# Attention's softmax by entire heads: scores of two heads in one five-bank PSUM tile, one maximum, one exponential and one scaling per head

## The chip, the cores and the metric

The kernel runs on one core of a Trainium2 chip. It is one launch of a long program (36247 instructions in the profiled execution) and the metric is its device time in microseconds (us), the median of three runs. Five engines work side by side and meet only at semaphores: TensorE (PE in the profile, with its weight loads as PEld), VectorE (DVE), ScalarE (ACT), GpSimd (POOL) and SyncE (SP, which only issues transfers here). Each works through its own instructions in the order in which they were written down. PSUM, into which TensorE writes, has eight banks of 512 fp32 numbers per partition.

## The reference, cut to what matters

The reference is a whole network block: a mixer with a state-space half and an attention half, a mixture of experts, then a second block. Only the attention is touched. It has 16 query heads and 4 key/value heads of 64 numbers, 1024 query positions and 256 + 1024 = 1280 key positions (context and latent), all in fp32:

```
q = rope(rms_norm(q));  k = [k_ctx, rope(rms_norm(k))];  v = [v_ctx, v]
for a block of 128 queries, for each of 16 heads (4 heads share one k, v):
    s = q . k                      # 128 x 1280
    p = exp(s - max(s)) / sum(exp(s - max(s)))
    o = p @ v
```

The result must be close to fp32, so the kernel holds most matrices as a sum of two fp32r numbers (a high and a low part), and multiplies both.

## The kernel before, in words

`attention` handles 8 blocks of 128 queries times 4 key heads, so 32 groups. A group has four query heads, that is two pairs of heads, and 10 chunks of 128 keys. The work is written as one loop over steps `s`, and in each step one piece of several stages is issued, each stage with its own distance from `s`; the loop runs under a manual schedule, so on TensorE, ScalarE, VectorE and GpSimd the written order is the executed order.

The front half runs ahead by `AHEAD` steps and is counted by `n = s + AHEAD`. Five values of `n` make a pair of heads, k = 0 to 4. `products` (L1135) writes the scores of piece k into a PSUM bank: pieces 0 and 1 are keys 0 to 511 and 512 to 1023 of the pair's first head, piece 2 holds the last 256 keys of both heads side by side in one bank, pieces 3 and 4 are keys 0 to 1023 of the second head. Each of the five banks is a tile of its own (S0 to S4). Each piece takes two matmuls (piece 2 four smaller ones), for the query's high and low parts. One step later `maxima` takes the maximum of that bank on VectorE (L1146 and L1148) and, at k = 2 and 4, the maximum over the head's three partial ones (L1155). Four steps after the product `exps` (L1170) computes the exponentials of the bank on ScalarE and sums them; GpSimd adds the three sums of a head (L1174, L1175). Five steps after it `norms` inverts the sum on VectorE (L1183) and scales the head's two halves on GpSimd (L1185).

The back half is counted by `s`, ten steps to a group. `transposes` (L1194) turns chunk `s + 2` of the four heads in one PSUM tile `pt` (two of them take turns); `high` (L1199, ScalarE) and `low` (L1203, VectorE) split it into two parts; `values` (L1215, L1216) multiplies both with v into the one bank `pv`. In a group's last step `evacuate` (L1223, L1224) copies `pv` out on ScalarE, and GpSimd adds its halves.

On TensorE a usual step is: products of piece k, transposes of a chunk, two matmuls of `values`. PSUM is full: five banks for scores, two for `pt`, one for `pv`.

Of the kernel before, what the change touches and what calls it, by code (L numbers as in the profile page):

```python
# [10 lines left out]
F = mybir.dt.float32  # L11
# [3 lines left out]
AF = mybir.ActivationFunctionType  # L15
OP = mybir.AluOpType
AX = mybir.AxisListType
# [5 lines left out]
L = 1024  # L23
S = 256
T = S + L
NB = L // 128
# [139 lines left out]
class Kernel:  # L166
# [126 lines left out]
    def conditioned(self, sm, s5_steps, zp, whp, wlp, wsp, toks):  # L293
# [11 lines left out]
        with es:  # L305
# [11 lines left out]
            for k in range(8):  # L317
# [35 lines left out]
    def proj_tok(self, sm):  # L353
# [10 lines left out]
        with es:  # L364
# [5 lines left out]
            s5_steps = self.s5_prepare(s5p, s5, pps)  # L370
            toks = [slice(S + tb * 128, S + tb * 128 + 128) for tb in range(NB)]
            wz, first = self.conditioned(sm, s5_steps, zp, whp, wlp, wsp, toks[:6])
# [14 lines left out]
            def product(wt, tok):  # L387
                return products(wt, [tok])[0]
# [113 lines left out]
            for hb in range(2):  # L502
                wt = load_block(1 + hb)
                for tb in range(NB):
                    ps = product(wt, slice(S + tb * 128, S + tb * 128 + 128))
                    next(mod)
# [596 lines left out]
    def attention(self):  # L1103
        nc, tc = self.nc, self.tc
        V = nc.vector
        self.o_es = ExitStack()
        op = self.o_es.enter_context(tc.tile_pool(name="oT", bufs=1, reuse_waits="tile"))
        self.oT = oT = [op.tile([128, 8, 128], F, name=f"oT{b}") for b in range(NB)]
        es = ExitStack()
        with es:  # L1110
            pool = lambda name, bufs=1, **kw: es.enter_context(tc.tile_pool(name=name, bufs=bufs, reuse_waits="tile", **kw))
            wp, cp, pp = pool("at_w", 2), pool("at_c"), pool("at_ps", 1, space=PS)
            kS, qS = self.kS, self.qS
            vS = cp.tile([128, NBT, 512], R, name="vS")
            nc.sync.dma_start(vS[:].bitcast(F), self.vv[:].rearrange("b p n -> p b n").bitcast(F))

            PIECES = (((0, 0, 512),), ((0, 512, 1024),), ((0, 1024, 1280), (1, 1024, 1280)), ((1, 0, 512),), ((1, 512, 1024),))
            AHEAD = 17
            NG = 4 * NB
            P, split, pvs, bank = {}, {}, {}, {}  # L1120
            mx, neg, tot, rt = {}, {}, {}, {}

            def products(n):

                pair, k = divmod(n, 5)
                b, j, p = pair // 8, pair % 8 // 2, pair % 2
                if pair >= 2 * NG:
                    return
                if n % 40 == 30 and b + 1 < NB:
                    self.load_q(b + 1)  # L1130
                S = bank[n] = pp.tile([128, 512], F, name=f"S{k}")
                o = 0
                for e, a, z in PIECES[k]:
                    for m in range(2):
                        nc.tensor.matmul(S[:, o:o + z - a], qS[b][:, 4 * j + 2 * p + e, :], kS[4 * m + j][:, a:z], start=m == 0, stop=m == 1)  # L1135
                    o += z - a

            def maxima(n):
                pair, k = divmod(n, 5)
                if n < 0 or pair >= 2 * NG:  # L1140
                    return
                if k == 0:
                    mx[pair] = wp.tile([128, 2, 3], F, name="mx")
                m = mx[pair]
                if k == 2:
                    V.tensor_reduce(m[:, :, 2], bank[n].rearrange("p (e n) -> p e n", e=2), axis=AX.X, op=OP.max)  # L1146
                else:
                    V.tensor_reduce(m[:, k // 3, k % 3:k % 3 + 1], bank[n], axis=AX.X, op=OP.max)  # L1148
                if k in (2, 4):
                    e = k // 2 - 1  # L1150
                    h = 2 * pair + e

                    hd = wp.tile([128, 8], F, name="hd", bufs=6)
                    neg[h], tot[h], rt[h] = hd[:, 0:1], hd[:, 1:4], hd[:, 4:6]
                    V.tensor_reduce(neg[h], m[:, e, :], axis=AX.X, op=OP.max, negate=True)  # L1155

            def exps(n):

                pair, k = divmod(n, 5)
                if n < 0 or pair >= 2 * NG:  # L1160
                    return
                o = 0
                for e, a, z in PIECES[k]:
                    h = 2 * pair + e
                    half = int(a > 0)
                    if (h, half) not in P:
                        P[h, half] = wp.tile([128, 768 if half else 512], F, name=f"P{half}", bufs=9 if half else 6)
                    i = k - 2 * e
                    x = P[h, half][:, a - 512 * half:z - 512 * half]
                    nc.scalar.activation(x, bank[n][:, o:o + z - a], AF.Exp, bias=neg[h], accum_out=tot[h][:, i:i + 1])  # L1170
                    o += z - a
                    if k == 2 + 2 * e:
                        r = rt[h]
                        nc.gpsimd.tensor_add(r[:, 0:1], tot[h][:, 0:1], tot[h][:, 1:2])  # L1174
                        nc.gpsimd.tensor_add(r[:, 1:2], r[:, 0:1], tot[h][:, 2:3])  # L1175

            def norms(n):
                pair, k = divmod(n, 5)
                if n < 0 or pair >= 2 * NG or k not in (2, 4):
                    return  # L1180
                h = 2 * pair + k // 2 - 1
                r = rt[h]
                V.reciprocal(r[:, 0:1], r[:, 1:2])  # L1183
                for half in range(2):
                    nc.gpsimd.tensor_scalar(P[h, half], P[h, half], r[:, 0:1], 1.0, op0=OP.mult, op1=OP.mult)  # L1185

            def transposes(n):
                g, c = divmod(n, NBT)
                if n < 0 or g >= NG:
                    return  # L1190
                pt = pp.tile([128, 4, 128], F, name="pt", bufs=2)
                o = 128 * (c - 4 if c > 3 else c)
                for i in range(4):
                    nc.tensor.transpose(pt[:, i, :], P[4 * g + i, int(c > 3)][:, o:o + 128], self.ident)  # L1194
                split[n] = pt, wp.tile([128, 4, 128], R, name="ph", bufs=4), wp.tile([128, 4, 128], R, name="pl", bufs=4)

            def high(n):
# [31 lines left out]
            with tc.manual_schedule(engines={ET.PE, ET.Activation, ET.DVE, ET.Pool}):  # L1229
                for s in range(-AHEAD, NBT * NG):  # L1230
                    n = s + AHEAD
                    last = s >= 0 and s % NBT == NBT - 1
                    if last:
                        values(s)
                    products(n)
                    maxima(n - 1)
                    transposes(s + 2)
                    low(s + 1)
                    exps(n - 4)
                    if last:  # L1240
                        evacuate(s)
                    norms(n - 5)
                    high(s + 2)
                    if not last:
                        values(s)
# [1466 lines left out]
```

## Time and profile before

| | |
|---|---|
| median of 3 runs | 2743.65 us (2742.18 to 2745.04) |
| profiled execution, its own time | 2740.33 us |
| its span, first to last instruction | 2738.4 us |
| mean granted TensorE clock | 0.959 |
| busy: TensorE, VectorE, ScalarE, GpSimd | 2536.7, 1951.2, 1336.1, 976.5 us |
| attention, first score product to last copy of `pv` | 800 to 1295 us |

The attention takes about 18% of the span. Busy times of matmuls overlap, since they are pipelined; so how fast TensorE moves is better read from the distance between the starts of matmuls than from their durations. Idle time stands in brackets in the timeline, with the instruction that ended it. `[0.43 <-ACT P L1170]` is 0.43 us in which the engine did nothing until an exponential was done.

### The profile page before, as it was taken

What the parts mean: (1) busy time and instruction counts of PE and PEld (TensorE: products, weight loads), DVE (VectorE), ACT (ScalarE), POOL (GpSimd) and SP (SyncE); (2) the same over time, 40 slices, a digit from 0 to 9 for tenths busy, and PEclk for the clock granted to TensorE, in tenths of its full rate; (3) what the DMA queues carried; (4) which work ended last, traced back from release to release, by engine and by line L of the source; (5) the groups of instructions that cost most, each with busy time, mean ns of one, the idle gap of its engine ahead of it and who ended that gap; (6) DMA issues with size and microseconds to landing.
All of it is one profiled execution on the core that took longest, in us unless ns stands there. A gap on an engine that the chain in (4) does not pass through costs nothing.

```text
span 2738.4 us, 36247 instructions
## 1 busy us (share of the span) xinstructions
PE 2536.7 (93%) x12369; PEld 2000.4 (73%) x12369; DVE 1951.2 (71%) x3735; ACT 1336.1 (49%) x2788; POOL 976.5 (36%) x1128
## 2 busy tenths in 40 slices
PE   7899999998899999998997999689799999999898
PEld 4676778854677777776775777577577788887787
DVE  7655676689649898897566777675647878775755
ACT  3233453456529999998223455343444333333433
POOL 5612011166016666666334455100241345443000
PEclk9999999988999999999987999899899999999999
DMA  7556421000610000002317788631312445547653
GB/s 270 175 189 204 155 71 39 32 8 1 245 62 17 17 17 32 17 1 69 116 70 221 223 263 264 215 109 46 112 54 74 164 148 184 173 159 269 232 196 116
DMA packets 141113, 344.21 MB, mean 126 GB/s; under 512 B 21200, under 2 KB 41344, under 8 KB 132064
## 3 DMA queue, kind: packets, MB, share of 16 engines
q1 hardware_dynamic: 88752, 198.03, 21.0%
q0 software_dynamic: 24176, 102.39, 11.5%
q10 hardware_dynamic: 28000, 41.46, 4.4%
q8 instruction: 98, 1.61, 0.2%
q14 instruction: 87, 0.71, 0.1%
HBM read 257.64 MB, written 93.62 MB: 128 GB/s over the span
## 4 chain that ended last, share of the span: by engine, by line
PE 64%; DVE 16%; ACT 7%; DMA 6%; issue 5%; POOL 2%; SPq 0%; ACTq 0%; DVEq 0%; POOLq 0%
PE m L217 5%; PE mm L215 5%; PE m L215 5%; PE m L216 5%; PE mm L217 5%; PE mm L216 5%; PE S L1135 5%; PE pt L1194 4%; PE a L216 3%; PE a L217 3%; PE a L215 2%; ACT P L1170 2%; PE pv L1215 2%; PE pv L1216 2%; PE cv L216 2%
## 5 line engine op out<-in xcount | busy, mean ns | idle before, releaser
L1203 DVE TENSOR_TENSOR pl<-pt,ph 128x512 fp32r<-128x512 f32 x320 | 219.1, 685 | 51.7 <-ACT ph L1199 46.3
L1170 ACT ACTIVATE P<-S,hd 128x512 f32<-128x512 f32 (+1 forms) x384 | 238.0, 624 | 1.8 <-DVE hd L1155 1.8
L1185 POOL TENSOR_SCALAR P<-P,hd 128x512 f32<-128x512 f32 (+1 forms) x256 | 202.7, 805 | 90.1 <-DVE hd L1183 85.5
L1135 PE MATMUL S<-kS,qS 128*128 128x512 f32 (+1 forms) x768 | 210.9, 372 | 19.1 <-ACT P L1170 19.1
L1199 ACT CAST ph<-pt 128x512 fp32r<-128x512 f32 x320 | 187.7, 587 | 28.0 <-PE pt L1194 14.5
L1194 PE MATMUL pt<-consts,P 128*128 128x128 f32 x1280 | 193.5, 273 | 6.0 <-DVE pl L1203 4.9
L1194 PEld LDWEIGHTS pt<-consts,P 128*128 128x128 f32 x1280 | 156.6, 140 | 45.2 <-DVE pl L1203 8.9
L1148 DVE TENSOR_REDUCE mx<-S 128x1 f32<-128x512 f32 x256 | 173.6, 679 | 3.0 <-PE S L1135 2.2
L1135 PEld LDWEIGHTS S<-kS,qS 128*128 128x128 f32 x768 | 128.3, 190 | 63.9 <-ACT P L1170 42.9
L1215 PE MATMUL pv<-ph,vS 128*128 128x512 f32 x320 | 151.3, 473 | 0.9 <-ACT ph L1199 0.3
L600 DVE SCALAR_TENSOR_TENSOR acc<-cv,vcol,acc 128x254 f32<-128x254 f32 (+5 forms) x288 | 110.3, 432 | 51.6 <-ACT acc L602 49.2
L2632 ACT CAST oh<-st 128x1024 fp32r<-128x1024 f32 x77 | 80.5, 1053 | 109.8 <-PE a L217 41.9
L216 PE MATMUL a<-ol,oh 128*128 128x512 f32 x308 | 122.0, 396 | 10.9 <-DVE ol L2633 10.9
L2633 DVE TENSOR_TENSOR ol<-st,oh 128x1024 fp32r<-128x1024 f32 x77 | 93.4, 1235 | 52.0 <-ACT oh L2632 45.1
L1216 PE MATMUL pv<-pl,vS 128*128 128x512 f32 x320 | 126.8, 396 | 0.2 <-DVE pl L1203 0.2
L217 PE MATMUL a<-oh,ol 128*128 128x512 f32 x308 | 121.7, 395 | 0.0
L215 PE MATMUL a<-oh 128*128 128x512 f32 x308 | 117.3, 391 | 0.3 <-DVE u L2550 0.3
L2440 ACT CAST gh<-gst 128x512 fp32r<-128x512 f32 x88 | 54.6, 621 | 128.1 <-PE m L216 122.0
L216 PE MATMUL mm<-wl,hH 128*128 128x512 f32 x288 | 114.6, 398 | 2.2 <-DVE wl L255 2.0
L215 PE MATMUL mm<-wh,hH 128*128 128x512 f32 x288 | 115.4, 401 | 0.0
L217 PE MATMUL mm<-wh,hL 128*128 128x512 f32 x288 | 113.5, 394 | 0.0
L217 PE MATMUL cv<-hH,wl 128*128 128x512 f32 (+1 forms) x288 | 104.0, 361 | 1.0 <-POOL wl L584 1.0
(785 smaller groups left out, 7494.5 us busy)
## 6 DMA issues: line engine op xcount, KB each, us to landing
gst<-in_ffn_gu_dram SPq DMA_DIRECT2D x88, 256.0 KB, 3.3
st<-hop SPq DMA_DIRECT2D x77, 256.0 KB, 7.4
wmod<-in_w_mod_dram ACTq DMA_DIRECT2D x64, 256.0 KB, 4.0
hop<-h POOLq DMA_DIRECT2D x44, 256.0 KB, 2.6
d<-in_ffn_down_dram SPq DMA_DIRECT2D x22, 512.0 KB, 3.5
wop<-d POOLq DMA_DIRECT2D x22, 512.0 KB, 3.5
st<-wop SPq DMA_DIRECT2D x44, 256.0 KB, 5.0
wst<-in_w_in_dram SPq DMA_DIRECT2D x40, 256.0 KB, 3.6
```

The costliest lines, as they stand in the source:

```text
L215: nc.tensor.matmul(out, lh, rh, start=first, stop=False)
L216: nc.tensor.matmul(out, lh, rl, start=False, stop=False)
L217: nc.tensor.matmul(out, ll, rh, start=False, stop=last)
L1135: nc.tensor.matmul(S[:, o:o + z - a], qS[b][:, 4 * j + 2 * p + e, :], kS[4 * m + j][:, a:z], start=m == 0, stop=m == 1)
L1148: V.tensor_reduce(m[:, k // 3, k % 3:k % 3 + 1], bank[n], axis=AX.X, op=OP.max)
L1170: nc.scalar.activation(x, bank[n][:, o:o + z - a], AF.Exp, bias=neg[h], accum_out=tot[h][:, i:i + 1])
L1185: nc.gpsimd.tensor_scalar(P[h, half], P[h, half], r[:, 0:1], 1.0, op0=OP.mult, op1=OP.mult)
L1194: nc.tensor.transpose(pt[:, i, :], P[4 * g + i, int(c > 3)][:, o:o + 128], self.ident)
L1199: nc.scalar.copy(split[n][1], split[n][0])
L1203: V.tensor_sub(split[n][2], split[n][0], split[n][1])
L1215: nc.tensor.matmul(pv, v, ph, start=c == 0, stop=False)
L1216: nc.tensor.matmul(pv, v, pl, start=False, stop=c == NBT - 1)
```

## The change

The five tiles for scores become one tile `S` of five banks, 128 x 2 x 1280: the two heads of a pair lie behind each other without gaps, so the first head fills banks 0, 1 and half of 2, and the second the rest. The pieces are cut along the banks, so there are as many matmuls of the same sizes as before. `maxima` is now one reduction over 1280 numbers per head (L1145), negated at once; `exps` is one activation over 1280 numbers with one sum (L1151), so GpSimd has no sums to add; `norms` is one inverse (L1156) and one scaling of 1280 numbers (L1157). The probabilities of a head are one tile, eight of them in turn. The maximum comes one step, the exponential two, and the scaling three steps after the head's last product, and the loop starts 16 steps ahead instead of 17.

```diff
-            PIECES = (((0, 0, 512),), ((0, 512, 1024),), ((0, 1024, 1280), (1, 1024, 1280)), ((1, 0, 512),), ((1, 512, 1024),))
-            AHEAD = 17
+            PIECES = (((0, 0, 512),), ((0, 512, 1024),), ((0, 1024, 1280), (1, 0, 256)), ((1, 256, 768),), ((1, 768, 1280),))
+            S = pp.tile([128, 2, T], F, name="S")
+            AHEAD = 16
...
-                S = bank[n] = pp.tile([128, 512], F, name=f"S{k}")
...
+                        nc.tensor.matmul(S[:, e, a:z], qS[b][:, 4 * j + 2 * p + e, :], kS[4 * m + j][:, a:z], start=m == 0, stop=m == 1)
+            def head(n):
+                pair, k = divmod(n, 5)
+                return None if n < 0 or pair >= 2 * NG or k not in (2, 4) else 2 * pair + k // 2 - 1
             def maxima(n):
+                h = head(n)
+                if h is not None:
+                    cols[h] = wp.tile([128, 8], F, name="hd", bufs=6)
+                    V.tensor_reduce(cols[h][:, 0:1], S[:, h % 2], axis=AX.X, op=OP.max, negate=True)
             def exps(n):
+                h = head(n)
+                if h is not None:
+                    P[h] = wp.tile([128, T], F, name="P", bufs=8)
+                    nc.scalar.activation(P[h], S[:, h % 2], AF.Exp, bias=cols[h][:, 0:1], accum_out=cols[h][:, 1:2])
             def norms(n):
+                h = head(n)
+                if h is not None:
+                    V.reciprocal(cols[h][:, 2:3], cols[h][:, 1:2])
+                    nc.gpsimd.tensor_scalar(P[h], P[h], cols[h][:, 2:3], 1.0, op0=OP.mult, op1=OP.mult)
...
-                    exps(n - 4)
+                    exps(n - 2)
...
-                    norms(n - 5)
+                    norms(n - 3)
```

How the instructions stand and what they wait for changes at three places. In the rows below the text in brackets names the engine whose semaphore the instruction waits for, and rows without one wait for nothing new. First TensorE near the start of the attention, before any transposes, so that the score products stand alone: piece 3 of the first pair is the first row, then come piece 4 and pieces 0, 1 and 2 of the second pair. Before (S_7131 is the tile of piece 3, S_7137 of piece 4, then S_7143, S_7151 and S_7161 for the next pair):

```order
L1135 MATMUL S_7131<-kS_6341,qS 128x512 [waits DVE_49]
L1135 MATMUL S_7131<-kS_6345,qS 128x512
L1135 MATMUL S_7137<-kS_6341,qS 128x512
L1135 MATMUL S_7137<-kS_6345,qS 128x512
L1135 MATMUL S_7143<-kS_6341,qS 128x512 [waits Activation_49]
L1135 MATMUL S_7143<-kS_6345,qS 128x512
L1135 MATMUL S_7151<-kS_6341,qS 128x512 [waits Activation_49]
L1135 MATMUL S_7151<-kS_6345,qS 128x512
L1135 MATMUL S_7161<-kS_6341,qS 128x256 [waits Activation_49]
```

The same place on TensorE now, with the one tile S:

```order
L1133 MATMUL S<-kS_6341,qS 128x512
L1133 MATMUL S<-kS_6345,qS 128x512
L1133 MATMUL S<-kS_6341,qS 128x512 [waits DVE_49]
L1133 MATMUL S<-kS_6345,qS 128x512
L1133 MATMUL S<-kS_6341,qS 128x512 [waits Activation_49]
L1133 MATMUL S<-kS_6345,qS 128x512
L1133 MATMUL S<-kS_6341,qS 128x512 [waits DVE_49]
L1133 MATMUL S<-kS_6345,qS 128x512
L1133 MATMUL S<-kS_6341,qS 128x256 [waits Activation_49]
```

Before, a product waited for the exponential that had read its own bank. Now pieces 4 and 1 wait for VectorE, and pieces 0 and 2 for ScalarE. Counting the semaphore's increments in the built program gives which instruction each waits for: piece 4 the maximum of the first head, piece 0 the exponential of the first head, piece 1 the maximum of the second head, piece 2 the exponential of the second head; in each case the reader of S that was issued in the step just before.

Second, VectorE in the steady part, five steps each. Before (S_8221 is a piece 2, S_8243 and S_8263 pieces 3 and 4):

```order
L1146 TENSOR_REDUCE mx<-S_8221 128x2 [waits PE_49]
L1155 TENSOR_REDUCE hd<-mx 128x1 [waits DVE_49]
L1203 TENSOR_TENSOR pl<-pt,ph 128x512 [waits Activation_49]
L1148 TENSOR_REDUCE mx<-S_8243 128x1 [waits PE_49]
L1203 TENSOR_TENSOR pl<-pt,ph 128x512 [waits Activation_49]
L1183 RECIPROCAL hd<-hd 128x1 [waits Pool_49]
L1148 TENSOR_REDUCE mx<-S_8263 128x1 [waits PE_49]
L1155 TENSOR_REDUCE hd<-mx 128x1 [waits DVE_49]
L1203 TENSOR_TENSOR pl<-pt,ph 128x512 [waits Activation_49]
L1148 TENSOR_REDUCE mx<-S_8283 128x1 [waits PE_49]
```

VectorE now, from the maximum of a first head on:

```order
L1145 TENSOR_REDUCE hd<-S 128x1 [waits PE_49,Pool_49]
L1174 TENSOR_TENSOR pl<-pt,ph 128x512 [waits DVE_49,Activation_49]
L1174 TENSOR_TENSOR pl<-pt,ph 128x512 [waits Activation_49]
L1145 TENSOR_REDUCE hd<-S 128x1 [waits PE_49,Activation_49,Pool_49]
L1174 TENSOR_TENSOR pl<-pt,ph 128x512 [waits DVE_49,Activation_49]
L1156 RECIPROCAL hd<-hd 128x1
L1174 TENSOR_TENSOR pl<-pt,ph 128x512 [waits DVE_49,Activation_49] x2
L1156 RECIPROCAL hd<-hd 128x1
```

Two reductions per pair stand where seven stood. The first head's maximum waits for TensorE, and the count says for which product: piece 3 of its pair, which lies in the second head. The second head's maximum waits for piece 0 of the next pair, and for ScalarE, namely the exponential of the first head.

Third, ScalarE in the steady part. Before, from the first exponential of a second head on (S_8329 is a piece 2):

```order
L1170 ACTIVATE P_8408,hd<-S_8329,hd 128x256
L1170 ACTIVATE P_8429,hd<-S_8329,hd 128x256 [waits DVE_49,Pool_49]
L1199 CAST ph<-pt 128x512 [waits PE_49,Activation_49]
L1170 ACTIVATE P_8448,hd<-S_8352,hd 128x512
L1199 CAST ph<-pt 128x512 [waits PE_49,Activation_49]
L1170 ACTIVATE P_8429,hd<-S_8372,hd 128x512
L1199 CAST ph<-pt 128x512 [waits DVE_49,PE_49]
```

ScalarE now, the five steps of a pair:

```order
L1151 ACTIVATE P,hd<-S,hd 128x1280 [waits DVE_49,PE_49]
L1170 CAST ph<-pt 128x512 [waits PE_49,Activation_49] x2
L1151 ACTIVATE P,hd<-S,hd 128x1280 [waits DVE_49,PE_49]
L1170 CAST ph<-pt 128x512 [waits PE_49,Activation_49] x2
L1170 CAST ph<-pt 128x512 [waits DVE_49,PE_49]
```

Six exponentials of a pair became two. Before, they waited for no product; now the first head's waits for piece 4 of its pair, and the second head's for piece 1 of the next pair. Outside the attention the engines' instructions are the same, but for the places of two weight casts on ScalarE and of one block of matmuls in the projection that follows.

## Rows read from the trace of the kernel before

**Rows 1.** Busy time by engine in the steady attention (columns: stretch, engines, clock, DMA).
```profile
820.00:1270.00 450.00, 436.73 (x2548) 352.08 (x2546) 403.69 (x851) 423.59 (x1091) 278.66 (x546) 1.00 0.05 15
```
**Rows 2.** Who waited for whom, 800 to 1300 us: total us, times, longest.
```profile
PE S L1135 <- ACT P L1170: 19.1, 35, 3.8
...
PE pt L1194 <- DVE pl L1203: 4.9, 5, 3.1
```
**Rows 3.** The line of the score products: ns min/median/max, first and last start.
```profile
L1135 PE MATMUL S<-kS,qS x768: 278/393/795, 800.3 to 1267.9; 128*128 128x512 f32 x128, 128*128 128x256 f32 x64
```
**Rows 4.** Timeline of two steps without a wait (start us, us, engine, line).
```profile
1004.58 0.73 PE L1135 MATMUL S<-kS,qS 128*128 128x256 f32 x4
...
1005.14 0.60 PE L1194 MATMUL pt<-consts,P 128*128 128x128 f32 x4
...
1005.84 0.59 ACT L1199 CAST ph<-pt 128x512 fp32r<-128x512 f32 x1 [0.17 <-PE pt L1194]
...
1006.05 0.63 PE L1135 MATMUL S<-kS,qS 128*128 128x512 f32 x2
...
1007.42 0.62 PE L1135 MATMUL S<-kS,qS 128*128 128x512 f32 x2
```
**Rows 5.** Timeline where a score product waits for an exponential.
```profile
1013.02 0.69 ACT L1170 ACTIVATE P<-S,hd 128x512 f32<-128x512 f32 x1
...
1013.60 0.20 ACT L1170 ACTIVATION_READ_ACCUMULATOR P<-S,hd 128x1 f32 x1
...
1013.85 0.72 PE L1135 MATMUL S<-kS,qS 128*128 128x512 f32 x2 [0.43 <-ACT P L1170]
...
1014.77 0.47 PE L1215 MATMUL pv<-ph,vS 128*128 128x512 f32 x1
...
1015.08 0.39 PE L1216 MATMUL pv<-pl,vS 128*128 128x512 f32 x1
```
**Rows 6.** Groups by shape, 800 to 1296 us: count, busy us, mean ns, idle before.
```profile
L1148 DVE TENSOR_REDUCE mx<-S 128x1 f32<-128x512 f32 x256 | 173.6, 679 | 3.0 <-PE S L1135 2.2
...
L1155 DVE TENSOR_REDUCE hd<-mx 128x1 f32<-128x3 f32 x128 | 20.0, 156 | 4.4
...
L1170 ACT ACTIVATE P<-S,hd 128x512 f32<-128x512 f32 x256 | 178.2, 696 | 1.5 <-DVE hd L1155 1.5
...
L1170 ACT ACTIVATE P<-S,hd 128x256 f32<-128x256 f32 x128 | 59.9, 478 | 0.3 <-DVE hd L1155 0.3
...
L1185 POOL TENSOR_SCALAR P<-P,hd 128x768 f32<-128x768 f32 x128 | 117.0, 914 | 0.0
L1185 POOL TENSOR_SCALAR P<-P,hd 128x512 f32<-128x512 f32 x128 | 89.2, 697 | 90.1 <-DVE hd L1183 85.5 <-PE S L1135 1.7
```
**Rows 7.** Timeline where TensorE waits for VectorE.
```profile
1272.03 0.69 DVE L1203 TENSOR_TENSOR pl<-pt,ph 128x512 fp32r<-128x512 f32 x1 [0.71 <-ACT ph L1199]
...
1272.78 0.66 PE L1194 MATMUL pt<-consts,P 128*128 128x128 f32 x4 [0.28 <-DVE pl L1203]
```
**Rows 8.** Timeline of the attention's start.
```profile
800.26 2.47 PE L1135 MATMUL S<-kS,qS 128*128 128x512 f32 x12
...
802.26 1.28 DVE L1148 TENSOR_REDUCE mx<-S 128x1 f32<-128x512 f32 x2
...
804.41 1.28 ACT L1170 ACT_TABLE_LOAD   x1 [25.12 <-DVE hd L1155]
...
806.54 3.94 PE L1135 MATMUL S<-kS,qS 128*128 128x512 f32 x12 [3.81 <-ACT P L1170]
```
**Rows 9.** Timeline of the attention's end.
```profile
1267.69 0.63 PE L1135 MATMUL S<-kS,qS 128*128 128x512 f32 x2
...
1268.35 26.17 SPq L979 DMA_DIRECT2D wst<-in_w_out_dram  x7
...
1294.17 0.58 ACT L1223 COPY lo<-pv 64x512 f32<-64x512 f32 x1 [0.52 <-POOL wl L983]
```
**Rows 10.** Busy time by engine in stretches with gaps on TensorE (first after the span: PE).
```profile
812.00:820.00 8.00, 5.76 (x28) 3.65 (x29) 6.33 (x15) 5.99 (x19) 5.76 (x12) 1.00 0.00 0
...
1920.00:1924.00 4.00, 2.44 (x6) 1.08 (x6) 1.44 (x2) 4.00 (x6) 1.09 (x1) 0.78 0.00 0
1924.00:1928.00 4.00, 3.28 (x7) 2.25 (x8) 3.99 (x6) 1.46 (x3) 2.40 (x3) 0.50 0.33 101
1928.00:1932.00 4.00, 4.00 (x16) 3.20 (x15) 3.91 (x4) 1.31 (x2) 4.00 (x2) 0.86 0.26 85
```

More of the change, by code (lines that the diff above doesn't have):

```diff
@@ L1115, in attention @@
             nc.sync.dma_start(vS[:].bitcast(F), self.vv[:].rearrange("b p n -> p b n").bitcast(F))
-            PIECES = (((0, 0, 512),), ((0, 512, 1024),), ((0, 1024, 1280), (1, 1024, 1280)), ((1, 0, 512),), ((1, 512, 1024),))
-            AHEAD = 17
+            PIECES = (((0, 0, 512),), ((0, 512, 1024),), ((0, 1024, 1280), (1, 0, 256)), ((1, 256, 768),), ((1, 768, 1280),))
+            S = pp.tile([128, 2, T], F, name="S")
+            AHEAD = 16
             NG = 4 * NB
-            P, split, pvs, bank = {}, {}, {}, {}
-            mx, neg, tot, rt = {}, {}, {}, {}
+            P, split, pvs, cols = {}, {}, {}, {}
             def products(n):
@@ L1130, in products @@
                     self.load_q(b + 1)
-                S = bank[n] = pp.tile([128, 512], F, name=f"S{k}")
-                o = 0
                 for e, a, z in PIECES[k]:
                     for m in range(2):
-                        nc.tensor.matmul(S[:, o:o + z - a], qS[b][:, 4 * j + 2 * p + e, :], kS[4 * m + j][:, a:z], start=m == 0, stop=m == 1)
-                    o += z - a
+                        nc.tensor.matmul(S[:, e, a:z], qS[b][:, 4 * j + 2 * p + e, :], kS[4 * m + j][:, a:z], start=m == 0, stop=m == 1)
@@ L1138, in maxima @@
+            def head(n):
+                pair, k = divmod(n, 5)
+                return None if n < 0 or pair >= 2 * NG or k not in (2, 4) else 2 * pair + k // 2 - 1
             def maxima(n):
[L1139 to L1155, printed above, removed]
-            def exps(n):
[L1159 to L1175, printed above, removed]
@@ L1177, in norms @@
-            def norms(n):
[L1178 to L1185, printed above, removed]
+                h = head(n)
+                if h is not None:
+                    cols[h] = wp.tile([128, 8], F, name="hd", bufs=6)
+                    V.tensor_reduce(cols[h][:, 0:1], S[:, h % 2], axis=AX.X, op=OP.max, negate=True)
@@ L1191, in transposes @@
                 pt = pp.tile([128, 4, 128], F, name="pt", bufs=2)
-                o = 128 * (c - 4 if c > 3 else c)
                 for i in range(4):
-                    nc.tensor.transpose(pt[:, i, :], P[4 * g + i, int(c > 3)][:, o:o + 128], self.ident)
+                    nc.tensor.transpose(pt[:, i, :], P[4 * g + i][:, 128 * c:128 * c + 128], self.ident)
                 split[n] = pt, wp.tile([128, 4, 128], R, name="ph", bufs=4), wp.tile([128, 4, 128], R, name="pl", bufs=4)
```

## The prediction

> **What bounds the kernel now.** I first read the busy times of the steady attention [rows 1]: TensorE 436.7 of 450 us at full clock, ScalarE 423.6, VectorE 403.7, GpSimd 278.7. TensorE is the bound, two engines are close behind. The list of waits comes next [rows 2]: TensorE idles 19.1 us for exponentials and 4.9 us for VectorE, little in an attention of 490 us. The line of the score products gives the pace [rows 3]: 64 pairs of heads between the first start at 800.3 and the last at 1267.9 us, so 467.6 / 64 = 7.31 us a pair. The timeline shows what a step is when nothing waits [rows 4]: from one product to the next 1007.42 - 1006.05 = 1.37 us, and 1006.05 - 1004.58 = 1.47 us where the piece has four matmuls. The five steps of a pair are thus about 7 us of TensorE, and the rest is waits, most of them where a group ends [rows 5]. Before, a product waits for an exponential issued only one step earlier as well, but that one is 512 wide and mostly early; everything else has steps of slack.
>
> **The part of the change that decides.** The order rows show that the scores are now one tile to the program, and that each reader of it waits for the write issued last, each write for the read issued last, whichever head they touch. So four of the five steps of a pair become a relay on the one tile, with nothing of it running beside the next leg:
>
> - piece 3, then the first head's maximum, which waits for piece 3 though that belongs to the other head;
> - piece 4, which waits for that maximum, then the first head's exponential, which waits for piece 4;
> - piece 0 of the next pair, which waits for this exponential, then the second head's maximum;
> - piece 1, which waits for that maximum, then the second head's exponential; piece 2 waits for it.
>
> Behind each waiting product stand, on TensorE's in-order queue, the step's transposes and `values`. They can't fill the gap; they run only after the product, beside the next maximum or exponential.
>
> The legs, each from a row:
>
> - A released pair of 512-wide products ends 0.72 us after its start [rows 5], an unreleased one 0.63 [rows 4].
> - TensorE to reader: 1005.14 + 0.60 = 1005.74, the cast starts at 1005.84 [rows 4]: 0.10, and I take 0.09 for the rounding.
> - Maximum over 1280: 156 ns at 3 elements and 679 at 512 [rows 6] give 1.028 ns an element, so 679 + 768 x 1.028 = 1.47 us. Bounds: 1280 x 1.028 = 1.32 without a fixed part, 2.5 x 679 ns = 1.70 if each bank costs a full one.
> - Exponential over 1280 with its sum: from the start of a 512 one to the end of its accumulator read are 1013.80 - 1013.02 = 0.78 us [rows 5]; an element costs (696 - 478) / 256 = 0.852 ns [rows 6], so 0.78 + 768 x 0.852 ns = 1.43 us. Bounds: 1280 x 0.852 ns = 1.09 plus the 0.09 that the read sticks out, 1.18; and 2.5 x 0.78 = 1.95.
> - Reader to TensorE: 1013.80 to 1013.85 = 0.05 from ScalarE [rows 5]; 1272.72 to 1272.78 = 0.06 from VectorE [rows 7].
>
> I take the slopes, because both lie between measured sizes of the same instruction. Then, from the start of one step's product to the next:
>
> - piece 2: no wait behind it, 1.47 us [rows 4]
> - piece 3: 0.63 + 0.09 + 1.47 + 0.06 = 2.25 us
> - piece 4: 0.72 + 0.09 + 1.43 + 0.05 = 2.29 us
> - piece 0: 0.72 + 0.09 + 1.47 + 0.06 = 2.34 us
> - piece 1: 2.29 us
>
> That is 10.64 us a pair against 7.31. The rest of a step's work hides: after a released product TensorE is done with transposes and `values` 1015.47 - 1013.85 = 1.62 us later [rows 5], within 2.29. VectorE's `low`, now behind a maximum, ends some 0.6 us into the next step, when the transposes that need its buffer are about due; they may slip 0.2 us inside the gap. ScalarE's cast behind an exponential ends 0.55 us into the next step, a step before its user.
>
> **What is removed, and what it is worth.** Per pair VectorE loses seven reductions for two (5 x 0.68 + 2 x 0.16 against 2 x 1.47: 0.7 us), ScalarE six activations for two (4 x 0.70 + 2 x 0.48 against 2 x 1.35: 1.0 us, and four accumulator reads), GpSimd four sums and a start of the scaling per head (697 + 914 ns become 697 + 768 x 0.85 = 1.35 us) [rows 6]. None of these sets the pace now, and in the relay only the length of one maximum and one exponential counts. The copies of `pv` at a group's end, which delayed an exponential before [rows 5], fall on a step whose ScalarE has none; worth nothing beyond the 10.64. The scaling ends over a step before the transposes that read it.
>
> **The sum.** Start: before, the second pair's piece 0 starts at 806.54, after the table load of 804.41 [rows 8]. Now the first maximum can start near 802.4 (piece 3 done, VectorE free), piece 4 follows, then load and exponential: about 807.0. From there 62 pairs x 10.64 = 659.7 us to piece 0 of the last pair; less 1.4 us because two early steps have no transposes, plus 0.5 for the slow clock at the start: 1465.8. Then 2.34 + 2.29 + 1.47 + 2.25 = 8.35 to the last product: 1474.2, where before it stood at 1267.7 [rows 9]. The shift is 206.5 us. What follows hangs on that product: the load of the next weights starts at its end [rows 9] and takes the same 26 us to the last copy of `pv`; the step that `AHEAD` saves lies beside that load, and I count it as nothing (it could give 1.4 us). The two casts and the block of matmuls that change places later I also put at nothing, within 5 us either way. 2740.3 + 206.5 = 2946.8 in the profiled execution's own time, which is 3.3 us under the median of the runs; so a median of **2950 us**.
>
> **Rivals.**
>
> *The clock falls.* TensorE would be busy (4 x 1.62 + 1.47) / 10.64 = 75% of the time, in gaps of some 0.7 us. At 812 to 820 us, with 72% and similar gaps, the rows show a clock of 1.00; at 1920 to 1924, with 61%, it is 0.78, then 0.50, the lower of its levels (1.2 of 2.4 GHz), and when TensorE was busy throughout it came back [rows 10]. The new stage lies on the good side of both, not far. At half the clock a step's TensorE work is at most 2 x 1.37 = 2.74 us, the relay legs grow by at most the 0.72 us of their products, to some 3.0, and piece 2 to 2.94: 14.9 us a pair. But then TensorE is busy nearly all the time, and [rows 10] show the clock return from that; I let half of the pairs be slow: 64 x 4.3 / 2 = 138 us more, 3088. The Trainium skill ("TensorE: Matmul & The Clock Gate", section "A second HAM failure mode: psum-queue depth-cycling") says that short idling between groups of matmuls which cycle through PSUM banks can make the clock swing between its two levels; by that rule this rival's time would come out, and the stretch at 812 us does not agree with it while the one at 1920 does.
>
> *The banks still pass singly (faster).* If a product waited only for readers of its own bank, the first head's chain from piece 2 to the next piece 0 would be 0.75 + 0.09 + 1.47 + 0.03 + 1.43 + 0.05 = 3.8 us, and TensorE has 1.47 + 1.37 + 1.37 = 4.2 us of steps for it. The gaps would close and a pair cost 4 x 1.37 + 1.47 = 6.95 us: 64 x 0.36 = 23 us off, 2721. It turns on one thing: whether pieces 4 and 1 wait for the other head's maximum. The order rows say they wait for VectorE, and no other instruction of VectorE touches S. The Trainium skill ("PSUM — Partial Sum Buffer", section "PSUM bank collisions raise a hardware error") asks that engines be kept apart by bank and quadrant only; by that alone this rival would hold, and the built program waits for more.
>
> *Each bank costs a full instruction.* With the upper bounds a pair takes 2 x (0.23 + 0.52) = 1.5 us more: 96 us, 3046. With the lower ones 2 x (0.15 + 0.25) = 0.8 less: 51 us, 2899.
>
> **How the numbers follow.** The relay at full clock 0.86, with its own range 2915 to 2985 (0.13 us a leg of four, 33 us); the falling clock 0.06; lengths near the upper bounds 0.04; banks singly 0.03; something that leaves the time alone 0.01. The range leaves most of the rivals' far ends out: 2910 to 3010. A difference under 0.2%, about 5.5 us, could not be told from none; all cases but the last two are far above it: slower 0.96, same 0.01, faster 0.03.
>
> **What would show it.** Score products every 10.6 us a pair; the longest waits of TensorE on its products, near 0.7 us each and 256 of them, half ended by VectorE's maximum, half by ScalarE's exponential; a maximum near 1.47 and an activation near 1.35 us; TensorE's busy share in the attention near 75% at clock 1.00; the last product near 1474 us. Wrong it would be if products waited for one engine alone, if the clock read under 0.95 there, or if either long instruction missed its slope.

## The result and the profile after

The changed kernel takes 2970.29 us in the median of four runs (2965.21 to 2973.86), the kernel before beside it 2744.35: a ratio of 1.0823, 95% interval 1.0806 to 1.084. Forecast were 2950 us and a range of 2910 to 3010. The profiled execution took 2969.4 us, its span 2967.6 against 2738.4.

First the line of the score products, in the form of [rows 3], and the busy times of the attention, in that of [rows 1]:

```profile
L1133 PE MATMUL S<-kS,qS x768: 274/396/797, 808.4 to 1489.9; 128*128 128x512 f32 x128, 128*128 128x256 f32 x64
```
```profile
820.00:1490.00 670.00, 511.49 (x2578) 339.54 (x2578) 381.94 (x554) 373.28 (x615) 210.60 (x185) 0.98 0.03 10
```

The products now last 681.5 us where they lasted 467.6. TensorE is busy 511.49 / 670 = 76% of the time in place of 97%, and the other engines less as well: nobody is the bound any more. The waits (total us, times, longest) say who waits for whom:

```profile
ACT P L1151 <- PE S L1133: 176.2, 126, 5.0
PEld S L1133 <- DVE hd L1145: 166.3, 127, 2.4
DVE hd L1145 <- PE S L1133: 165.7, 96, 4.2
...
PE S L1133 <- DVE hd L1145: 116.0, 127, 1.7
PEld S L1133 <- ACT P L1151: 104.2, 126, 2.5
...
PE S L1133 <- ACT P L1151: 48.8, 95, 2.1
```

TensorE waits for both of the others, and both of the others wait for TensorE. (Rows of PEld are the weight loads of the same products, so their times are not to be added to those of PE.) In [rows 2] only the exponentials stood before a product, with 19.1 us. The relay itself is to be read in the timeline of one pair:

```profile
1006.01 0.74 PE L1133 MATMUL S<-kS,qS 128*128 128x256 f32 x4 [0.46 <-ACT P L1151]
...
1007.49 0.62 PE L1133 MATMUL S<-kS,qS 128*128 128x512 f32 x2
...
1008.22 1.49 DVE L1145 TENSOR_REDUCE hd<-S 128x1 f32<-128x1280 f32 x1 [0.99 <-PE pt L1165]
...
1009.77 0.74 PE L1133 MATMUL S<-kS,qS 128*128 128x512 f32 x2 [0.74 <-DVE hd L1145]
...
1010.54 1.33 ACT L1151 ACTIVATE P<-S,hd 128x1280 f32<-128x1280 f32 x1 [1.37 <-PE S L1133]
...
1011.77 0.19 ACT L1151 ACTIVATION_READ_ACCUMULATOR P<-S,hd 128x1 f32 x1
...
1012.02 0.73 PE L1133 MATMUL S<-kS,qS 128*128 128x512 f32 x2
...
1012.88 1.49 DVE L1145 TENSOR_REDUCE hd<-S 128x1 f32<-128x1280 f32 x1 [1.97 <-PE S L1133]
...
1014.42 0.73 PE L1133 MATMUL S<-kS,qS 128*128 128x512 f32 x2 [1.25 <-DVE hd L1145]
...
1015.19 1.34 ACT L1151 ACTIVATE P<-S,hd 128x1280 f32<-128x1280 f32 x1 [1.08 <-PE S L1133]
...
1016.67 0.74 PE L1133 MATMUL S<-kS,qS 128*128 128x256 f32 x4 [0.48 <-ACT P L1151]
```

Piece 2 at 1006.01 has all of the first head's scores written at 1006.75, and VectorE is idle for the 0.99 us before 1008.22; yet the maximum starts only when piece 3, of the other head, has ended at 1008.11. (The profile puts this idle time down to the transposes, which were under way then; by the semaphore counts in the section on the change it is piece 3 that the maximum waits for.) Piece 4 starts 0.06 us after the maximum, the exponential 0.03 us after piece 4, and so on to piece 2 of the next pair: 1016.67 - 1006.01 = 10.66 us, where two pairs took 6.91 and 7.93 before.

The maximum, the scaling and the exponential by themselves, and the transposes, from 820 to 1490 us (count, busy us, mean ns, idle before), beside [rows 6]:

```profile
L1165 PE MATMUL pt<-consts,P 128*128 128x128 f32 x1220 | 187.9, 277 | 0.0
L1145 DVE TENSOR_REDUCE hd<-S 128x1 f32<-128x1280 f32 x125 | 186.4, 1491 | 193.1 <-PE S L1133 160.5 <-PE pt L1165 32.6
...
L1157 POOL TENSOR_SCALAR P<-P,hd 128x1280 f32<-128x1280 f32 x125 | 167.1, 1337 | 306.6 <-DVE hd L1156 301.5 <-ACT ph L1170 2.0 <-POOL oT L1198 0.3
L1151 ACT ACTIVATE P<-S,hd 128x1280 f32<-128x1280 f32 x125 | 166.1, 1329 | 174.9 <-PE S L1133 174.9
```

### The profile page after: what moved, and what is told of

Same layout as the page of the kernel before. It is cut to its first block, busy times and chain, and to the rows that moved or that the text cites. A ratio compares the mean times of both kernels' runs of the same rounds, so it can differ in the third digit from the quotient of the medians.

```text
span 2967.6 us, 35371 instructions
## 1 busy us (share of the span) xinstructions
PE 2611.5 (88%) x12369; PEld 1984.3 (67%) x12369; DVE 1924.3 (65%) x3415; ACT 1276.5 (43%) x2276; POOL 900.0 (30%) x744
## 4 chain that ended last, share of the span: by engine, by line
PE 60%; DVE 21%; issue 6%; ACT 6%; DMA 5%; POOL 2%; DVEq 0%; SPq 0%; POOLq 0%; ACTq 0%
PE S L1133 8%; DVE hd L1145 6%; PE mm L215 5%; PE mm L217 5%; PE mm L216 4%; PE m L217 4%; PE m L215 4%; PE m L216 4%; ACT P L1151 3%; PE a L216 2%; PE a L217 2%; PE a L215 2%; PE pt L1165 2%; DMA u<-yo,tab 2%; PE cv L216 2%
## 5 line engine op out<-in xcount | busy, mean ns | idle before, releaser
L1133 PE MATMUL S<-kS,qS 128*128 128x512 f32 (+1 forms) x768 | 233.4, 401 | 165.6 <-DVE hd L1145 116.0
L1145 DVE TENSOR_REDUCE hd<-S 128x1 f32<-128x1280 f32 x128 | 190.9, 1491 | 199.5 <-PE S L1133 165.7
L1133 PEld LDWEIGHTS S<-kS,qS 128*128 128x128 f32 x768 | 118.5, 194 | 277.2 <-DVE hd L1145 166.3
L1157 POOL TENSOR_SCALAR P<-P,hd 128x1280 f32<-128x1280 f32 x128 | 171.2, 1337 | 422.6 <-DVE hd L1156 416.6
L1174 DVE TENSOR_TENSOR pl<-pt,ph 128x512 fp32r<-128x512 f32 x320 | 211.7, 680 | 98.0 <-ACT ph L1170 98.0
L1151 ACT ACTIVATE P<-S,hd 128x1280 f32<-128x1280 f32 x128 | 170.1, 1329 | 176.9 <-PE S L1133 176.2
L1165 PEld LDWEIGHTS pt<-consts,P 128*128 128x128 f32 x1280 | 148.7, 141 | 69.5 <-issue 45.0
```

The lines of the kernel that those rows point to most:

```text
L1133: nc.tensor.matmul(S[:, e, a:z], qS[b][:, 4 * j + 2 * p + e, :], kS[4 * m + j][:, a:z], start=m == 0, stop=m == 1)
L1145: V.tensor_reduce(cols[h][:, 0:1], S[:, h % 2], axis=AX.X, op=OP.max, negate=True)
L1151: nc.scalar.activation(P[h], S[:, h % 2], AF.Exp, bias=cols[h][:, 0:1], accum_out=cols[h][:, 1:2])
L1157: nc.gpsimd.tensor_scalar(P[h], P[h], cols[h][:, 2:3], 1.0, op0=OP.mult, op1=OP.mult)
L1165: nc.tensor.transpose(pt[:, i, :], P[4 * g + i][:, 128 * c:128 * c + 128], self.ident)
L1174: V.tensor_sub(split[n][2], split[n][0], split[n][1])
```

## The experiments

The theory was that waits on the tile as a whole make the relay. Its chief rival was width: two readers of 1280 columns are simply too long for five banks. Ten kernels were run.

### The narrow instructions on one tile

```
+            SS = pp.tile([128, 5, 512], F, name="S")
...
-                S = bank[n] = pp.tile([128, 512], F, name=f"S{k}")
+                S = bank[n] = SS[:, k]
```

> The kernel before with its narrow maxima, exponentials and lags, but its five one-bank tiles declared as one tile of five banks. Theory (one tile makes a relay, whatever the width): the built program now makes each product wait for the last exponential issued, each maximum for the last product, and each exponential even for the last maximum; so a step is product 0.72 + 0.09 + maximum 0.68 + 0.04 + exponential 0.78 + 0.05 = 2.36 us, the fifth about 2.7: 12.1 us a pair against 7.31, 2744 + 64 x 4.8 = 3050 us (2980 to 3100), slower than the wide kernel. Rival 'width': narrow instructions cost what they cost before, 7.3 us a pair, about 2745.

Measured: 3063.3 us, one run; pairs of 11.97 and 12.15 us in turn. One step in its timeline:

```profile
1009.95 0.74 PE L1136 MATMUL S<-kS,qS 128*128 128x256 f32 x4 [0.93 <-ACT P L1171]
1010.73 0.69 DVE L1149 TENSOR_REDUCE mx<-S 128x1 f32<-128x512 f32 x1 [1.29 <-PE S L1136]
1011.46 0.69 ACT L1171 ACTIVATE P<-S,hd 128x512 f32<-128x512 f32 x1 [1.08 <-DVE mx L1149]
1012.04 0.19 ACT L1171 ACTIVATION_READ_ACCUMULATOR P<-S,hd 128x1 f32 x1
1012.29 0.30 PEld L1136 LDWEIGHTS S<-kS,qS 128*128 128x128 f32 x2 [1.13 <-ACT P L1171]
```

```profile
900.00:1000.00 100.00, 68.54 (x347) 45.56 (x346) 57.58 (x116) 59.38 (x152) 37.74 (x74) 1.00 0.03 11
```

The second fence is a stretch of the same kernel (columns: us, then TensorE, its weight loads, VectorE, ScalarE, GpSimd, and the clock). The three engines work on different pieces in different banks, and still each starts when the one before it ends. One declaration costs 317 us over the kernel before (2746.78 us beside it), more than the whole change did: in the changed kernel the wide instructions soften the relay, since they have fewer legs. The rival of width, as it was put for this run, falls.

### Only the foreign waits dropped

Tile, widths and order stay; the waits between accesses that share no bank go (`free` drops one, `after` sets one).

```
+                other = (2 * pair - 1,) if k < 2 else (2 * pair,) if k > 2 else ()
+                for h in other:
+                    for x in (mx.get(h), ex.get(h)):
...
+                                free(w, x)
...
+            def late(x, h, n):
+                for i in (n + 1, n + 2):
+                    for w in mm.get(i, ()):
+                        free(x, w)
+                after(x, mm[n][-1])
```

> The changed kernel with its instructions, widths and order as they are; only the waits between accesses of S that share no bank are dropped (pieces 3 and 4 no longer wait for the first head's maximum and exponential, pieces 0 and 1 of the next pair no longer for the second head's; a maximum or exponential waits for the last piece of its own head). Theory (the relay comes from waits on the tile as a whole): the gaps of 0.74 us before four of five products close, TensorE's own steps (4 x 1.37 + 1.47 = 6.95 us) or at most ScalarE and VectorE set the pace, 7.0 to 7.4 us a pair instead of 10.65, so about 64 x 3.4 = 218 us less: 2735 us, range 2715 to 2770. Rival 'width' (the two readers of 1280 columns are too long for the five banks, whatever waits for them): the pair stays above 10 us and the time above 2900.

Measured: 2788.1 us (2785.62 to 2793.4), 1.0143 of before, interval 1.0115 to 1.017. Of the 226 us, 182 are back, so width alone is not what costs them. But the pair takes 7.75 and 8.02 us in turn, 7.89 in the mean, not 7.0 to 7.4, and the time lies above the range that was expected. The products run on beside the maximum:

```profile
1007.03 1.47 DVE L1165 TENSOR_REDUCE hd<-S 128x1 f32<-128x1280 f32 x1
...
1007.38 0.62 PE L1141 MATMUL S<-kS,qS 128*128 128x512 f32 x2
...
1008.75 0.63 PE L1141 MATMUL S<-kS,qS 128*128 128x512 f32 x2
```

Half of the foreign waits at a time was tried next. **Only the readers freed** (the edit without the lines on `other`):

> The changed kernel; only the maxima and exponentials are freed from pieces of the other head (each waits for the last piece of its own head), while the products keep all their waits, the ones for the other head's maximum too. Theory (it is the reader's wait for a piece that it does not read that makes the relay; a maximum started at once is done before piece 4 or piece 1 is due): close to the run with all foreign waits dropped, 7.9 to 8.2 us a pair, 2788 to 2815 us. Rival (the products' waits for the other head's maximum cost the larger part): 9 us a pair or more, above 2860.

Measured: 2776.14 us, one run, the same 7.75 and 8.02 us a pair. **Only the products freed** (the edit without `late`):

> The other half: pieces 3, 4, 0 and 1 are freed from the other head's readers, while each maximum and exponential still waits for the product issued last. Theory: from piece 3's start 0.62 + 0.10 + maximum 1.49 + 0.04 + exponential with its read 1.42 + 0.05 to piece 0, then 0.73 + 0.10 + 1.49 + 0.04 + 1.42 + 0.05 to piece 2, then 1.47: 9.0 us a pair, up to 9.6 where casts and subtractions stand ahead; 2970 - 64 x 1.35 = 2884 us (2860 to 2905). Rival (as above): below 2815.

Measured: 2886.24 us, one run, 9.20 and 9.66 us a pair. The second is as the theory had it, the first 12 us under it; that is not the edit's, for from first to last product it takes 500.3 us beside 499.1 with both freed, and its first product starts at 799.1 us instead of 809.8. Either half opens the ring, but not equally: freeing the readers gives all that freeing both gave, freeing the products 84 us of it. A product that waits for the other head's maximum loses little once that maximum starts in time.

### The maximum twice

```
+                    for _ in range(2):
+                        V.tensor_reduce(cols[h][:, 0:1], S[:, h % 2], axis=AX.X, op=OP.max, negate=True)
```

> The changed kernel with each maximum computed twice, the same result written over itself. Theory (the maximum is a leg of the relay at its full length): 128 x 1.49 = 191 us more, 2970 + 191 = 3161 us (3140 to 3180), the pair 13.6 us. Rival (TensorE or ScalarE sets the pace and VectorE, busy 57%, has room for part of it): under 100 us more, below 3070.

Measured: 3254.39 us, one run: 284 us more, not 191. The pair takes 14.37 and 16.35 us in turn. The maximum is indeed on the path at its full length, but something came on top. A stretch of it, and two products from its timeline:

```profile
1200.00:1300.00 100.00, 69.06 (x278) 49.80 (x278) 59.72 (x74) 39.49 (x65) 22.95 (x20) 0.78 0.03 11
```
```profile
1211.34 0.73 PE L1133 MATMUL S<-kS,qS 128*128 128x512 f32 x2
...
1215.28 1.22 PE L1133 MATMUL S<-kS,qS 128*128 128x512 f32 x2 [2.77 <-DVE hd L1146]
```

After gaps of 2.8 us the product took 1.22 us in all 28 cases, after gaps of 2.3 us in 51 of 90: the granted clock falls toward the lower of its two levels and comes back, again and again: each 100 us from 900 to 1600 have 0.77 to 0.81. From first to last product it is 968.6 us against 681.5, which is 287 more, 96 above the forecast. Most of these 96 us sit behind slow products: behind piece 1 the next product starts after 2.6 to 2.7 us instead of 2.24, in every second pair behind piece 4 too, and there behind piece 2 after 2.6 instead of 1.48 (means).

### Transposes in the first steps

```
+                    if s < -2:
+                        pt = pp.tile([128, 4, 128], F, name="pt", bufs=2)
+                        for i in range(8):
+                            nc.tensor.transpose(pt[:, i % 4, :], self.ident, self.ident)
```

> The changed kernel with eight transposes of the identity, which nobody reads, behind each product of the first 14 steps, where nothing else stands behind the products. Theory (the first four pairs take 12.0 instead of 10.65 us because TensorE's clock falls when only products run): the granted clock from 812 to 850 us is 1.00, those pairs take 10.7 us, the whole 4 to 8 us less, 2964 us. Rival (the first pairs are slow for another reason): the pairs stay at 12 us or get slower by the added work, 2970 or more.

Measured: 2956.76 us (2953.12 to 2964.84), 1.0767 of before, interval 1.0735 to 1.0799, which lies below that of the changed kernel. First the changed kernel's clock, then this one's, from 820 to 830 us:

```profile
820.00:830.00 10.00, 4.75 (x11) 2.59 (x12) 3.21 (x4) 1.87 (x4) 1.37 (x2) 0.50 0.00 0
```
```profile
820.00:830.00 10.00, 7.24 (x50) 5.75 (x48) 3.21 (x4) 2.44 (x4) 2.67 (x2) 1.00 0.00 0
```

Three pairs took 12.0 us each; with the transposes they take 10.52, 11.02 and 10.81, which is 3.6 us less, while the transposes delay the first maximum by some 2.6. (The clock was 1.00 from 812 to 850 us as expected, but for 0.83 from 830 to 840.) From first to last product it is 679.5 against 681.5 us. So the cause is right: the slow clock costs these pairs about 4 us, and the run as built gains 2 in the attention. The rest of the 13.5 us between the medians isn't the edit's as far as the profiles show: of the 10.3 us between the two profiled executions, 7.0 lie before the first product, mainly in the stretch from 600 to 700 us, whose clock was 0.83 in this profile and 0.78 in the other.

### What is left without foreign waits

The second head's maximum still waits for the first head's exponential, since both read bank 2. First suspect:

```
+            def scores(h):
+                if h % 2 == 0:
+                    return S[:, 0]
+                return S[:, 1, 256:896].unsqueeze(1).broadcast_to([128, 2, 640])
...
+                    if h % 2:
+                        free(mx[h], ex[h - 1])
```

> The run with the foreign waits dropped, and the second head's maximum and exponential read 640 columns of banks 3 and 4 twice (still 1280 columns each) in place of its own, so that the two heads' readers share no bank and the second maximum need not wait for the first exponential. It leaves out the second head's first 256 scores and its last 384. Theory (what still separates the 7.89 us a pair from the 7.42 of the kernel before is the bank that two heads share): 7.3 to 7.5 us a pair, 2755 us (2740 to 2768). Rival (casts, subtractions and reciprocals stand behind instructions of 1.3 to 1.5 us on in-order queues): still 7.7 to 7.9 us, 2775 to 2790.

Measured: 2799.73 us (2793.55 to 2813.88), 1.0201 of before, interval 1.016 to 1.0242, and the pair at 7.76 and 8.02 us what it was, to within a hundredth. The wait for the exponential is gone from the list and nothing is gained: the theory of the shared bank falls. (The whole time can't be set against the 2788 us: with other scores the later stages have 12,415 matmuls instead of 12,369.) The timeline of this kernel shows the loop that does set the pace:

```profile
1008.67 0.75 PE L1141 MATMUL S<-kS,qS 128*128 128x256 f32 x4 [0.84 <-ACT P L1179]
...
1011.25 0.59 ACT L1199 CAST ph<-pt 128x512 fp32r<-128x512 f32 x1 [0.72 <-PE pt L1194]
...
1011.74 1.34 ACT L1179 ACTIVATE P<-S,hd 128x1280 f32<-128x1280 f32 x1
...
1012.96 0.20 ACT L1179 ACTIVATION_READ_ACCUMULATOR P<-S,hd 128x1 f32 x1
...
1013.22 0.73 PE L1141 MATMUL S<-kS,qS 128*128 128x512 f32 x2 [0.15 <-ACT P L1179]
...
1014.47 0.59 ACT L1199 CAST ph<-pt 128x512 fp32r<-128x512 f32 x1 [0.83 <-PE pt L1194]
...
1014.96 1.34 ACT L1179 ACTIVATE P<-S,hd 128x1280 f32<-128x1280 f32 x1
...
1016.43 0.75 PE L1141 MATMUL S<-kS,qS 128*128 128x256 f32 x4 [0.22 <-ACT P L1179]
```

The exponential stands on ScalarE's queue behind the cast of the step before it; that cast waits for its step's transposes, which stand on TensorE behind its step's product; and the product of the step after waits for the exponential. 2.58 + 0.49 + 1.48 + 1.25 + 0.49 + 1.47 = 7.76 us, the pair. To test it, the two casts were taken off that queue:

```
+                    (V.tensor_copy if vec else nc.scalar.copy)(split[n][1], split[n][0])
...
+                    high(s + 2, n % 5 in (0, 3))
```

> The run with all foreign waits dropped, and two of a pair's five casts, those that stand on ScalarE right before an exponential, done by VectorE instead. Theory (the 7.76 us that remain are a loop through ScalarE's queue: piece 2 to cast 2.58, cast 0.49, exponential with its read 1.42, 0.06, piece 0 to cast 1.25, cast 0.49, exponential 1.42, 0.05): the two casts leave the loop, 7.1 to 7.4 us a pair, 2788 - 64 x 0.6 = 2750 us (2738 to 2768). Rival (VectorE, with two casts of 0.7 us more, becomes the bound): 7.7 us a pair or more, 2780 and above.

Measured: 2765.57 us (2761.52 to 2772.24), 1.0086 of before, interval 1.0055 to 1.0117; pairs of 7.53 and 7.66 us, not 7.1 to 7.4. The gain is there, at half its size. What took the other half stands in the busy times, and in the list of waits from 900 to 1200 us:

```profile
900.00:1100.00 200.00, 193.44 (x1109) 145.89 (x1109) 194.10 (x290) 129.26 (x210) 90.43 (x81) 1.00 0.05 17
```

```profile
ACT P L1172 <- DVE hd L1165: 62.7, 60, 1.5
```

VectorE is busy 194.1 of 200 us, and the exponentials, which in the same stretch of the run with the foreign waits dropped did not once wait for a maximum, now do so 60 times. The loop through ScalarE's queue was the bound, and VectorE is right behind it: both sides had a part.

### One part alone, and a layout of two-bank tiles

```
-                        P[h, half] = wp.tile([128, 768 if half else 512], F, name=f"P{half}", bufs=9 if half else 6)
+                        P[h] = wp.tile([128, T], F, name="P", bufs=8)
...
-                for half in range(2):
-                    nc.gpsimd.tensor_scalar(P[h, half], P[h, half], r[:, 0:1], 1.0, op0=OP.mult, op1=OP.mult)
+                nc.gpsimd.tensor_scalar(P[h], P[h], r[:, 0:1], 1.0, op0=OP.mult, op1=OP.mult)
```

> The kernel before with one part of the change alone: P is one tile for a head and GpSimd scales it in one instruction of 1280 instead of 512 and 768; banks, maxima and exponentials as before. Theory (GpSimd sets no pace; its shorter scaling is worth nothing): 2744 us within 0.3%. Rival (the scaling decides when the transposes may start, or fewer P buffers hold an exponential back): 5 to 20 us in either direction.

Measured: 2761.97 us (2755.82 to 2768.68), 1.005 of before, interval 1.0032 to 1.0067. The rival had it, and the list of waits names it:

```profile
ACT P L1169 <- PE pt L1191: 15.8, 30, 0.8
```

With 8 tiles for an entire head, an exponential that starts a new one waits, once in almost every group, for the transposes that still read the old one; the split tiles had let go of its first 512 columns earlier. The score products last 484.5 us instead of 467.6. The changed kernel has 8 such tiles too, but its list has no such wait: it runs one step less ahead, so the transposes come a step sooner beside the same exponential.

Last, wide instructions on tiles that belong to one head each:

```
+                if k in (0, 2, 3):
+                    bank[pair, k] = pp.tile([128, 512 if k == 2 else 1024], F, name=f"S{k}")
...
+                if k in (0, 3):
+                    nc.scalar.activation(P[h][:, :1024], bank[pair, k], AF.Exp, bias=neg[h], accum_out=tot[h][:, 0:1])
...
+                    norms(n - 5)
                     low(s + 1)
```

In this run the inverse of the sum also stands before `low` in a step, where it stood behind it before.

> The kernel before with the tiles cut so that no wait crosses heads: the first head's banks 0 and 1 are one tile of 1024 columns, bank 2 with both heads' last 256 scores its own tile, banks 3 and 4 the second head's tile; a maximum and an exponential of 1024 in place of two of 512, one scaling of 1280 for a head, 16 steps ahead. Theory (wide readers cost nothing where a tile's readers and writers belong to one head; they save ScalarE two starts and two accumulator reads, some 0.6 us a pair, so the copies of pv at a group's end no longer push the exponentials that a product waits for): 7.0 to 7.2 us a pair where before they take 6.91 and 7.93 in turn, 2725 us (2708 to 2742). Rival (an exponential of 1024 releases piece 0's bank later than one of 512 did, 1.2 instead of 0.8 us after its start, and a product waits for it in every pair): 7.6 us a pair or more, 2755 to 2780.

Measured: 2755.85 us (2745.46 to 2765.27), 1.0046 of before, interval 1.0024 to 1.0067. No relay, but no gain: the pairs take 7.36 and 7.57 us, 7.46 in the mean, beside 7.42 before. Busy times, and a row of the waits from 850 to 1280 us:

```profile
900.00:1100.00 200.00, 197.97 (x1128) 152.06 (x1127) 173.53 (x323) 169.09 (x375) 101.10 (x133) 1.00 0.07 22
```
```profile
PEld S L1137 <- ACT P L1169: 33.1, 85, 0.4
```

ScalarE did get its air (169.09 of 200 us instead of 188.31), yet TensorE counts as busy for 197.97. Its products still wait a little for an exponential, in most pairs, as the rival had it at a higher price: the wait shows on the weight loads, while the matmul behind counts 0.73 instead of 0.63 us as busy. From first to last product that is 471.6 against 467.6 us; what makes up the other 8 to 9 us of the median was not found, as the profiled execution was one of the fastest. So none of the ten beats the kernel before.

## Why the prediction was right, point by point

**The relay** stood as described, each of its legs and their order: shown by the timeline, and by taking away its cause in whole and in halves. From product to product, in the median over the attention, against the forecast: behind piece 2 1.48 (1.47), piece 3 2.28 (2.25), piece 4 2.24 (2.29), piece 0 2.41 (2.34), piece 1 2.24 us (2.29). The sum is 10.65 against 10.64; single legs were off by up to 0.07 us and their errors cancelled.

**The legs.** The maximum takes 1.491 us (forecast 1.47), the exponential with its read 1011.96 - 1010.54 = 1.42 (1.43): the slopes between two measured sizes held, and the bounds with a full instruction for each bank were far off. That rival is out.

**What hides** did: the transposes have no idle time before them, and `values` none. The two lists of waits are as forecast in kind: 127 times VectorE, 126 times ScalarE on the weight loads. On the matmuls most waits for VectorE are 0.74 to 0.79 us long and some 30 of the 127 about 1.25, and most of those for ScalarE 0.45 to 0.48.

**What is removed** sets no pace in the relay, as said: the legs add up without it. (Its two differences come to 0.8 and 1.1 us where the prediction has 0.7 and 1.0; nothing was built on them.) But the run with the scaling alone shows that the argument had a hole: one tile for a head is not free by itself where its buffers are short. That the changed kernel escapes this by its earlier transposes was not tried by itself; the run with tiles of two banks, with the same 8 tiles and 16 steps ahead, has no such wait either.

**The sum** is where the 20 us between 2950 and 2970 arose. The shift of the span is 2967.6 - 2738.4 = 229.2 us, forecast 206.5. From first to last product it is 681.5 - 467.6 = 213.9, so the attention was mis-sized by 7.4: "plus 0.5 for the slow clock at the start" is the term that failed. From the second pair on a product takes 1.22 us, and the clock stays at 0.50 till the transposes join. From 814.9 to 851.8 us three pairs, counted from piece 0 to piece 0, take 36.9 us where 3 x 10.64 - 1.4 + 0.5 = 31.0 were forecast: 5.9 of the 7.4, so that the term measured about 6.4 us. The start in the timeline of the changed kernel, beside [rows 8]:

```profile
808.39 2.14 PE L1133 MATMUL S<-kS,qS 128*128 128x512 f32 x10 [0.78 <-DVE u L1069]
...
812.13 1.28 ACT L1151 ACT_TABLE_LOAD   x1 [25.65 <-DVE hd L1145]
...
814.89 1.22 PE L1133 MATMUL S<-kS,qS 128*128 128x512 f32 x2 [2.06 <-ACT P L1151]
```

The first product is 8.1 us late: 0.78 of it is a wait for VectorE's `u` of the stage before, since the one tile can start only when all its banks are free (all nine profiles with the one tile have this wait, none of the three with separate tiles); the rest lies in the unchanged stretch before it, from 600 to 700 us, whose clock was 0.78 here and 0.86 in the profile of before, and 0.79 to 0.85 in others of this study. Those 7.3 us aren't the change's as far as the profiles show: with the one tile as well, the first product started anywhere from 799.1 to 810.4 us. The end has 7.2 us more, which the prediction put at nothing "within 5 us either way": 2.5 of them stand before the first matmul of the projection that follows (32.6 us behind the last product instead of 30.1); where the others arise was not tested. That the median came 20 us and not 23 above the forecast is luck: this profiled execution lay 0.9 us under the median of its runs, not 3.3.

**The falling clock** was given 0.06 and did not come in the steady attention (10.65 us a pair throughout), but the ground under it was thinner than "on the good side of both" suggests: it fell at the start, and with the maximum doubled it fell again and again. The Trainium skill's rule on it ("TensorE: Matmul & The Clock Gate", section "A second HAM failure mode: psum-queue depth-cycling"), by which short idling between groups of matmuls on cycling banks can make the clock swing, agrees with the trace of the doubled maximum, 0.77 to 0.83, and not with that of the narrow relay, 1.00.

**The banks that pass singly.** This rival could be built, by dropping the waits: it gives 2788 us where the prediction put it at 2721. The failing step is "the gaps would close and a pair cost 4 x 1.37 + 1.47": it followed the chain through the banks alone and left out the in-order queue of ScalarE, where the casts stand before the exponentials; taking two of the five casts off that queue brought the pair from 7.89 to 7.60 us. The Trainium skill ("PSUM — Partial Sum Buffer", section "PSUM bank collisions raise a hardware error") asks for order by bank and quadrant, reads against reads too; the run with foreign waits dropped keeps to that, and the run with separate banks shows that the read against read costs nothing here.

## What to carry to other kernels

In this program a tile is also the unit of waiting: before banks are joined into one, list for each access the access before it on another engine, whatever part it touches, and add up the ring that this makes. Price such a ring leg by leg from measured slopes, and follow every in-order queue that it passes, casts and copies included. When a part of a change "costs nothing", check the buffers behind it as well as the engines.

## What was not expected of the hardware

- TensorE busy 68.5 of 100 us in steps with gaps mostly of 0.7 to 0.9 us, none above 1.4, kept a clock of 1.00 (the narrow relay); busy 69.06 of 100 us with gaps of 2.3 to 2.8 us it had 0.78 (the doubled maximum). The busy share alone does not tell the clock.
- Eight transposes per step that nobody reads raised the clock of the first pairs from 0.50 to 1.00 (0.83 in one stretch of 10 us).
- A product that is let go late shows partly as busy time: 0.73 us instead of 0.63. TensorE read 99% busy in a kernel that was no faster than one with 97%.
